# Gating the spatial and convolution branches, and splitting the products, in the projection phase instead of in the output tiles

## The chip, the core and the metric

The kernel runs on one core of a Trainium2 chip. The metric is the time on the device in microseconds, from launch to end. TensorE does the matmuls, VectorE (DVE), ScalarE (ACT) and GpSimd (POOL) the elementwise work, and SyncE (SP) issues all DMAs but two gathers.

## The reference

A decoder step with two layers. Each layer modulates its input of 2048 prompt tokens and 64 sample tokens (1024 features), projects it to 13 slabs, and runs four branches of 256 features: A, differential attention; B, a spatial-gating MLP; C, a convolution with 31 taps, LayerNorm, swish and a pointwise matmul; D, a gated recurrence (HGRN2). Every branch has a gate of its own, and the four products go through one output projection:

```python
o_a = o_a * silu(ag)
o_b = gelu(bu) * mixed(gelu(bv)) * silu(bg)
o_c = conv(cin) * silu(cg)
o_d = rms_norm(hgrn(dq, df, di)) * silu(dg)
mixed = concatenate([o_a, o_b, o_c, o_d]) @ w_out
y = layer_norm(ALPHA * x + gate * mixed)
```

The matmuls keep the accuracy of fp32 by splitting each operand into a high part (a cast to fp32r) and a low part (what the cast left out), and adding three products: high by high, low by high, high by low.

## The kernel before

**Phases.** Each layer has a projection phase in two groups of 1024 tokens (g=0, which also takes the 64 sample tokens, and g=1), and after it a phase of attention and output tiles. In the trace layer 0 projects until about 1010 us, attends until about 1620 us, layer 1 projects until about 2580 us and attends to the end.

**What the projection phase leaves in DRAM.** Gates are computed with features on the partitions: a matmul into PSUM, a tanh on ACT, `gate2` on DVE (L195), a store. `gate_slab` (L862) does so for the gate of D, `gate_pair` (L874) for those of A and C, and both store into the DRAM tensor `gat`. `gate_b` (L888) forms gelu(u) times the gate of B on POOL (L901) and stores that to `gat` too. A group has its tokens in blocks of 512 (with the sample tokens as well: 512, 288 and 288). The spatial mix of B (`b_v`, L906) and the convolution (`c_taps`, L1014, 30 multiply-adds on DVE per block at L1026; then `c_norm`, L1032) store their outputs in the DRAM tensor `catT`, features on rows. `c_norm` ends with a pointwise matmul (L1065), an ACT copy from PSUM (L1067, recorded at the helper's line L110) and a store.

**Output tiles.** `out_tile` (L1326) runs 17 times per layer, for 16 tiles of 128 prompt tokens and one of the 64 sample tokens. It multiplies branches by gates, splits the product in two parts and does the output matmuls (L1373 to L1375: high, low weight, low part). Half 0 (A and D) loads rows of `cat`, transposes them on TensorE and multiplies from PSUM on DVE (L1355). Half 1 (B and C) loads 512 rows of `gat` and of `catT` and multiplies on POOL:

```python
load(f4(gt), S.gat[g][half * 512:(half + 1) * 512, c0:c0 + M]...)   # L1337
load(f4(ct), S.catT[g][:, c0:c0 + M]...)                             # L1341
pick('EOT').tensor_tensor(tmp[:, cs], ct[:, cs], gt[:, cs], ALU.mult)  # L1349, POOL
cpy('EOH', hi[:, cs], tmp[:, cs])                                    # L1356, ACT cast, recorded at L110
sub_lo(..., lo[:, cs], tmp[:, cs], hi[:, cs])                        # L1357, POOL, recorded at L172
```

Loads and products live in staging tiles of 512 columns, "os" (4 buffers) and "zs" (5 buffers). "os" is shared with the loads of x in `build_h` (L453), which prepares the input of the next group.

**What sets the order.** Tile's scheduler orders the instructions of each engine from the program, its dependences, the buffers and the priorities in a table (L92 to L97), so an edit in one place can move rows elsewhere. All loads and stores stand in the one queue of SP. K, Q, V, the raw rows of `w_out` (cast on ACT at L1306, low part on POOL) and the vectors of the output LayerNorm (L1390, L1391 on POOL) are loaded into pools that open when the projection's pools close.

Of the kernel before, what the change touches and what calls it, by code (L numbers as in the profile page):

```python
# [9 lines left out]
F32 = mybir.dt.float32  # L10
F32R = mybir.dt.float32r
# [13 lines left out]
P = 128  # L25
# [43 lines left out]
def hymba_step_kernel(  # L69
# [60 lines left out]
    pool = L()  # L130
    pool.T2, pool.t2 = None, False
    uid = [0]

# [112 lines left out]
    def layer_scratch(l):  # L246
        s = L()
        s.qs = [[dram.tile([256, TG], F32, name=f"q{h}{l}_{g}") for h in "hl"] for g in range(NG)]
        s.ks = [[dram.tile([256, TG], F32, name=f"k{h}{l}_{g}") for h in "hl"] for g in range(NG)]
        s.vs = [dram.tile([512, 256], F32, name=f"v{l}_{b}") for b in range(T // 512)]  # L250
        s.catT = [dram.tile([512, RW], F32, name=f"catT{l}_{g}") for g in range(NG)]
        s.cat = [dram.tile([512, 512], F32, name=f"cat{l}_{b}") for b in range(T // 512)]
        s.gat = [dram.tile([D, RW], F32, name=f"gat{l}_{g}") for g in range(NG)]
# [607 lines left out]

    def gate_slab(l, g, h, col, row):  # L862
        w = slab(l, [(col, 256)])
        for m in range(2):
            for c0, n in blocks(g):
# [4 lines left out]
                gate2(o[:, 0:n], o[:, 0:n], ps[:, 0:n])  # L870
                store(scr[l].gat[g][row + m * P:row + (m + 1) * P, c0:c0 + n], o[:, 0:n])
                yield
# [15 lines left out]
    def gate_b(l, g, h, half):  # L888
        c = half * P
        w = slab(l, [(O_BU + c, P), (O_BG + c, P)])  # L890
        for c0, n in blocks(g):
# [9 lines left out]
            nc.gpsimd.tensor_tensor(a, a, b, ALU.mult)  # L901
            store(scr[l].gat[g][512 + c:512 + c + P, c0:c0 + n], a)
            yield
# [128 lines left out]
    def c_norm_(l, g, C, acc, t0, n, smpl, Lx):  # L1032
# [29 lines left out]
            for m in range(2):  # L1062
# [3 lines left out]
                o = C.pool.tile([P, 512], F32, tag="cn", name=nm("cn"), bufs=4)  # L1066
                cpy('ECO', o[:, 0:n], ps[:, 0:n])  # L1067
                r = TG if smpl else t0
                store(scr[l].catT[g][256 + m * P:256 + (m + 1) * P, r:r + n], o[:, 0:n])

# [255 lines left out]
    def out_tile(l, ti, O, last=False, act=None):  # L1326
# [7 lines left out]
        for half in (1, 0) if last else (0, 1):  # L1334
            f4 = lambda x: x[:, 0:4 * M].rearrange("p (k t) -> p k t", k=4)
            gt = st("os")
            load(f4(gt), S.gat[g][half * 512:(half + 1) * 512, c0:c0 + M].rearrange("(k p) t -> p k t", p=P))  # L1337
            ct, tmp = st("os"), st("os")
            hi, lo = st("zs", F32R), st("zs", F32R)
            if half:  # L1340
                load(f4(ct), S.catT[g][:, c0:c0 + M].rearrange("(k p) t -> p k t", p=P))  # L1341
            elif last:
# [3 lines left out]
            for k0, k1 in ((2, 4), (0, 2)) if last and not half else ((0, 4),):  # L1346
                cs = slice(k0 * M, k1 * M)
                if half:
                    pick('EOT').tensor_tensor(tmp[:, cs], ct[:, cs], gt[:, cs], ALU.mult)  # L1349
                else:  # L1350
                    ps = zt()
                    src = act if last and k0 == 0 else ct
                    for k in range(k0, k1):
                        nc.tensor.transpose(ps[:, k * M:(k + 1) * M], src[0:M, k * P:(k + 1) * P], ident[0:M, 0:M])
                    nc.vector.tensor_tensor(tmp[:, cs], ps[:, cs], gt[:, cs], ALU.mult)  # L1355
                cpy('EOH', hi[:, cs], tmp[:, cs])  # L1356
                sub_lo(nc.vector if last and not half else pick('EOL'), lo[:, cs], tmp[:, cs], hi[:, cs])  # L1357
                parts += [(O_K[half * 4 + k], f4(hi)[:, k, :], f4(lo)[:, k, :]) for k in range(k0, k1)]
        x = []
# [49 lines left out]
    for l in range(DEPTH):  # L1409
        with ExitStack() as ctx2:  # L1410
# [3 lines left out]
            for g in range(NG):  # L1414
# [38 lines left out]
                with tc.tile_pool(name=nm("cn"), reuse_waits="tile", bufs=1) as C.pool:  # L1453
                    todo = [(b * 512, 512, False) for b in range(NB)] + ([(0, NS, True)] if g == 0 else [])
                    accs = [c_taps(C, *todo[0], Lx)]
                    if g == 0:
                        with tc.tile_pool(name=nm("sap"), reuse_waits="tile", bufs=1) as sap:
                            prio(PSA, attention_sample, l, Lx, Sx, sap)
                    prio(KN['PGB'], run, gate_b(l, g, h, 0), gate_b(l, g, h, 1))
                    def mods():  # L1460
# [36 lines left out]
                    if KN['MO'] == 2:  # L1497
                        mods()
                if not KN['CS']:
                    c_state(l, g, C)  # L1500
# [74 lines left out]
```

## Time and profile before

| | |
|---|---|
| median of 3 runs | 3169.99 us (3167.98 to 3174.93) |
| the profiled execution | 3160.83 us |
| its span | 3159.1 us |
| granted TensorE clock, mean | 0.951 of full speed |
| busy: PE, DVE, ACT, POOL | 2828.0, 2235.2, 1162.9, 960.8 us |
| DMA: bytes moved, mean rate | 441.31 MB, 140 GB/s |

The profile covers one execution, from its first to its last instruction. Busy times are sums over the span, so they average stages with different limits. "Line" is the line of the program; helpers (L110 copies and casts on ACT, L172 subtractions that form low parts, L166 loads, L169 stores) collect operations of many places, and the tile names tell them apart.

### The profile page before, as it was taken

Reading aid. Unit: us, or ns where it says so; the run is one execution under the profiler, and the core shown is the slowest. Engines: PE = TensorE matmul, PEld = TensorE weight load, DVE = VectorE, ACT = ScalarE, POOL = GpSimd, SP = SyncE. Lnnn points to the kernel's source line nnn. Section 1 sums busy time; section 2 is a strip of 40 time slices with the busy share of each in tenths; the row PEclk is TensorE's granted clock in tenths of the full one; section 3 lists DMA queues with packets and bytes.
Section 4 is the critical chain, followed back from the end, with each engine's and each line's share of the span. In section 5 each row is a group of like instructions: output and inputs, shape, how many; then the busy total and the mean of one; then the engine's idle time right before and its main releaser. Section 6 shows DMA issues by size and latency. Waiting matters only on the chain. (4 is left out here: it accounts for less than half of the span.)

```text
span 3159.1 us, 55749 instructions
## 1 busy us (share of the span) xinstructions
PE 2828.0 (90%) x20888; PEld 2254.7 (71%) x20888; DVE 2235.2 (71%) x5280; ACT 1162.9 (37%) x2452; POOL 960.8 (30%) x1061
## 2 busy tenths in 40 slices
PE   5999989898999798888979999999999988997986
PEld 3888876788876566656668888767888856665665
DVE  2567883367583788879956678833676749898897
ACT  3212223211112666666641112232110146567663
POOL 3344364312011233404253344552120031332232
PEclk8999999899999899989989999999999988998998
DMA  6433544323555754446453335444334355444652
GB/s 237 147 128 108 173 146 154 108 92 128 174 180 203 184 133 112 118 112 166 122 197 111 122 119 192 140 139 124 117 120 140 117 166 123 129 118 108 158 155 67
DMA packets 323263, 441.31 MB, mean 140 GB/s; under 512 B 58704, under 2 KB 207734, under 8 KB 315811
## 3 DMA queue, kind: packets, MB, share of 16 engines
q1 hardware_dynamic: 316850, 420.97, 44.0%
q0 software_dynamic: 6144, 16.79, 1.8%
q8 instruction: 165, 2.70, 0.4%
q14 instruction: 104, 0.84, 0.1%
HBM read 295.80 MB, written 142.05 MB: 139 GB/s over the span
## 5 line engine op out<-in xcount | busy, mean ns | idle before, releaser
L525 PE MATMUL z<-hh,wh 128*128 128x512 f32 (+1 forms) x1440 | 528.4, 367 | 17.1 <-DVE zs L195 9.1
L527 PE MATMUL z<-hh,wl 128*128 128x512 f32 (+1 forms) x1440 | 522.1, 363 | 0.0
L526 PE MATMUL z<-hl,wh 128*128 128x512 f32 (+1 forms) x1440 | 518.6, 360 | 0.0
L516 PE MATMUL z<-wh,hh 128*128 128x256 f32 (+1 forms) x1360 | 399.9, 294 | 16.0 <-ACT wh L110 4.3
L686 ACT ACTIVATE P<-S,stt 128x1024 f32<-128x1024 f32 (+7 forms) x384 | 332.7, 868 | 182.1 <-DVE stt L682 120.0
L518 PE MATMUL z<-wh,hl 128*128 128x256 f32 (+1 forms) x1360 | 394.7, 290 | 0.0
L517 PE MATMUL z<-wl,hh 128*128 128x256 f32 (+1 forms) x1360 | 393.9, 290 | 0.6 <-POOL wl L172 0.6
L682 DVE TENSOR_REDUCE stt<-S 128x1 f32<-128x1024 f32 (+7 forms) x384 | 344.0, 904 | 64.2 <-PE S L680 48.7
L1026 DVE SCALAR_TENSOR_TENSOR acc<-glu,cw,acc 128x512 f32<-128x512 f32 x480 | 378.0, 834 | 3.3
L525 PEld LDWEIGHTS z<-hh,wh 128*128 128x128 f32 x1440 | 275.7, 191 | 80.1 <-issue 14.4
L527 PEld LDWEIGHTS z<-hh,wl 128*128 128x128 f32 x1440 | 275.5, 191 | 44.7 <-issue 7.0
L526 PEld LDWEIGHTS z<-hl,wh 128*128 128x128 f32 x1440 | 275.7, 191 | 42.7 <-issue 6.3
L678 PE MATMUL S<-K,Q 128*128 128x512 f32 (+3 forms) x640 | 229.2, 430 | 77.1 <-ACT P L686 61.6
L516 PEld LDWEIGHTS z<-wh,hh 128*128 128x128 f32 (+1 forms) x1360 | 262.3, 193 | 25.9 <-issue 5.7
L517 PEld LDWEIGHTS z<-wl,hh 128*128 128x128 f32 (+1 forms) x1360 | 261.9, 193 | 4.9 <-issue 2.6
L518 PEld LDWEIGHTS z<-wh,hl 128*128 128x128 f32 (+1 forms) x1360 | 261.5, 192 | 2.3 <-issue 0.3
L172 POOL TENSOR_TENSOR wl<-raw,wh 128x512 fp32r<-128x512 f32 x112 | 150.8, 1362 | 256.5 <-ACT wh L110 218.2
L1373 PE MATMUL z<-woh,zs 128*128 128x512 f32 (+1 forms) x480 | 202.7, 422 | 24.0 <-ACT zs L110 15.1
L1375 PE MATMUL z<-woh,zs 128*128 128x512 f32 (+1 forms) x480 | 200.2, 417 | 10.0 <-POOL zs L172 9.8
L730 PE MATMUL X<-ph,V 128*64 128x128 f32 x2176 | 196.1, 294 | 10.4 <-ACT ph L727 9.8
L678 PEld LDWEIGHTS S<-K,Q 128*128 128x128 f32 x640 | 114.9, 204 | 122.1 <-ACT P L686 90.0
L725 PE MATMUL T<-cst,P 128*128 128x128 f32 x1088 | 189.2, 302 | 13.3 <-DVE P L707 8.8
(374 smaller groups left out, 5410.5 us busy)
## 6 DMA issues: line engine op xcount, KB each, us to landing
wp<-wh SPq DMA_DIRECT2D x28, 1024.0 KB
wp<-wl SPq DMA_DIRECT2D x28, 1024.0 KB
wh<-wp SPq DMA_DIRECT2D x56, 512.0 KB
wl<-wp SPq DMA_DIRECT2D x56, 512.0 KB
K<-kh SPq DMA_DIRECT2D x224, 128.0 KB
K<-kl SPq DMA_DIRECT2D x224, 128.0 KB
mw<-in_w_ada_dram SPq DMA_DIRECT2D x24, 1024.0 KB
raw<-in_w_in_dram SPq DMA_DIRECT2D x64, 256.0 KB
```

The source lines that it names most:

```text
L516: nc.tensor.matmul(ps, hh[:, k, tok:tok + M], wh[:, k, :], start=(k == 0), stop=False)
L517: nc.tensor.matmul(ps, hh[:, k, tok:tok + M], wl[:, k, :], start=False, stop=False)
L518: nc.tensor.matmul(ps, hl[:, k, tok:tok + M], wh[:, k, :], start=False, stop=(k == KT - 1))
L525: nc.tensor.matmul(ps, wh[:, k, ms], hh[:, k, c0:c0 + n], start=(k == 0), stop=False)
L526: nc.tensor.matmul(ps, wh[:, k, ms], hl[:, k, c0:c0 + n], start=False, stop=False)
L527: nc.tensor.matmul(ps, wl[:, k, ms], hh[:, k, c0:c0 + n], start=False, stop=(k == KT - 1))
L678: nc.tensor.matmul(s[:, o:o + w], qt[:, m, :], kst[pc * 2 + o // 512][:, m, 0:w], start=True, stop=not diag)
L682: nc.vector.tensor_reduce(col(m, pc), s[:, :n], AX.X, ALU.max, negate=True)
L686: nc.scalar.activation(p[:, :n], s[:, :n], AF.Exp, bias=col(m, pc), scale=1.0, accum_out=l1 if m == 0 and npc == 1 else col(m, 2 + pc))
L1026: nc.vector.scalar_tensor_tensor(av, src(j), Lx.cw[:, c, j:j + 1], av, op0=ALU.mult, op1=ALU.add)
L1373: nc.tensor.matmul(po[0:M], a, wh[:, k, :], start=(i == 0), stop=False)
L1375: nc.tensor.matmul(po[0:M], b, wh[:, k, :], start=False, stop=(i == KT - 1))
```

## The change

In each layer the product of branch and gate, and its split in two parts, is made once per block of the projection phase for B and C, and the parts go to new DRAM tensors `bc` (high and low). `gat` keeps the gates of A and D, `catT` the spatial mix, and `gc` holds the gate of C. `gate_b` loads the mix and multiplies on DVE; `c_norm` loads the gate of C and multiplies from PSUM on DVE, where ACT copied. Each then casts on ACT, subtracts on POOL and stores both parts. The gate of C is now computed ahead of those of A and D. In g=0 the parts are staged in "os"; in g=1 in a pool of their own, "tp", with 6 buffers. Half 1 of an output tile only loads two parts.

```diff
+    def tp_row(dt=F32):
+        return pool.tp.tile([P, 512], dt, tag="tp", name=nm("tp"), bufs=NTP) if pool.tp else st("os", dt)
+
+    def two_parts(l, g, r, c0, n, x):
+        hi, lo = tp_row(F32R)[:, 0:n], tp_row(F32R)[:, 0:n]
+        nc.scalar.copy(hi, x)
+        sub_lo(nc.gpsimd, lo, x, hi)
+        for part, dst in zip((hi, lo), scr[l].bc[g]):
+            store(dst[r:r + P, c0:c0 + n], part)
...
             nc.gpsimd.tensor_tensor(a, a, b, ALU.mult)
-            store(scr[l].gat[g][512 + c:512 + c + P, c0:c0 + n], a)
+            ct = tp_row()[:, 0:n]
+            load(ct, scr[l].catT[g][c:c + P, c0:c0 + n])
+            nc.vector.tensor_tensor(a, a, ct, ALU.mult)
+            two_parts(l, g, c, c0, n, a)
             yield
...
-                cpy('ECO', o[:, 0:n], ps[:, 0:n])
                 r = TG if smpl else t0
-                store(scr[l].catT[g][256 + m * P:256 + (m + 1) * P, r:r + n], o[:, 0:n])
+                load(o[:, 0:n], scr[l].gc[g][m * P:(m + 1) * P, r:r + n])
+                nc.vector.tensor_tensor(o[:, 0:n], ps[:, 0:n], o[:, 0:n], ALU.mult)
+                two_parts(l, g, 256 + m * P, r, n, o[:, 0:n])
...
         for half in (1, 0) if last else (0, 1):
...
             hi, lo = st("zs", F32R), st("zs", F32R)
             if half:
-                load(f4(ct), S.catT[g][:, c0:c0 + M].rearrange("(k p) t -> p k t", p=P))
+                for part, src in zip((hi, lo), S.bc[g]):
+                    load(f4(part), src[:, c0:c0 + M].rearrange("(k p) t -> p k t", p=P))
+                parts += [(O_K[4 + k], f4(hi)[:, k, :], f4(lo)[:, k, :]) for k in range(4)]
+                continue
...
+                    if g == NG - 1:
+                        ctx3 = ExitStack()
+                        pool.tp = ctx3.enter_context(tc.tile_pool(name=nm("tp"), reuse_waits="tile", bufs=1))
...
-                    gp = chain(gate_slab(l, g, h, *((O_DG, 256), (O_AG, 0), (O_CG, 768))[KN['GO']]), gate_pair(l, g, h, *(((O_AG, 0), (O_CG, 768)), ((O_DG, 256), (O_CG, 768)), ((O_AG, 0), (O_DG, 256)))[KN['GO']]))
+                    gp = chain(gate_c(l, g, h), gate_pair(l, g, h, (O_AG, 0), (O_DG, 256)))
```

`gate_c` is `gate_slab` cut to the gate of C, with its store to `gc`. The changed program's lines are numbered 1 to 21 higher.

**POOL, output tiles of layer 0.** Before, a tile has three rows: the low part of half 0 (`zs_13509`), the product of half 1 at L1349, and its low part (`zs_13524`); `x` rows are the LayerNorm of the tile before.

```order
406 L1390 TENSOR_TENSOR x_12031<-x_12031,lng_10813 128x512
407 L1391 TENSOR_TENSOR x_12031<-x_12031,lnb_10814 128x512
408 L172 TENSOR_TENSOR zs_13509<-os_13507,zs_13508 128x512
409 L1349 TENSOR_TENSOR os_13522<-os_13521,os_13519 128x512
410 L172 TENSOR_TENSOR zs_13524<-os_13522,zs_13523 128x512
411 L1390 TENSOR_TENSOR x_12116<-x_12116,lng_10813 128x512
```

```order
414 L1409 TENSOR_TENSOR x_12132<-x_12132,lng_10969 128x512
415 L1409 TENSOR_TENSOR x_12163<-x_12163,lng_10969 128x512
416 L1410 TENSOR_TENSOR x_12132<-x_12132,lnb_10970 128x512
417 L1410 TENSOR_TENSOR x_12163<-x_12163,lnb_10970 128x512
418 L173 TENSOR_TENSOR zs_13631<-os_13634,zs_13630 128x512
```

The same tile has one row now, the low part of half 0.

**SP, end of g=0 in layer 0.** `os` from `in_x_prompt_dram` are the loads of x for g=1; before, four of them come behind the convolution's store of the block.

```order
243 L169 DMA catT_0_142<-cn_6042 128x512
244 L169 DMA gat_0_148<-zs_6104 128x288
245 L166 DMA os_6162<-in_x_prompt_dram 128x512
246 L166 DMA os_6176<-in_x_prompt_dram 128x512
247 L169 DMA catT_0_142<-cn_6047 128x512
248 L166 DMA os_6189<-in_x_prompt_dram 128x512
```

```order
254 L167 DMA cn_6125<-gc_0_144 128x512
255 L170 DMA gat_0_150<-zs_6188 128x288
256 L170 DMA bch_0_152<-os_6117 128x512
257 L170 DMA bcl_0_153<-os_6118 128x512
258 L170 DMA bch_0_152<-os_6128 128x512
259 L167 DMA os_6192<-in_x_prompt_dram 128x512
260 L167 DMA os_6206<-in_x_prompt_dram 128x512
261 L170 DMA bcl_0_153<-os_6129 128x512
262 L167 DMA os_6219<-in_x_prompt_dram 128x512
```

Now the four "os" buffers hold the two parts of both rows of that block, and eight loads of x come behind their stores.

**SP, end of the projection in layer 1.** Before, half of the raw `w_out` rows are loaded between gate stores, ahead of the convolution's last stores.

```order
1103 L169 DMA gat_1_191<-zs_25989 128x512
1104 L166 DMA raw_26895<-in_w_out_dram 128x512
1105 L166 DMA raw_26899<-in_w_out_dram 128x512
1112 L166 DMA raw_26923<-in_w_out_dram 128x512
1113 L169 DMA catT_1_185<-cn_26059 128x512
```

```order
1201 L170 DMA bcl_1_203<-tp_26322 128x512
1202 L170 DMA bch_1_202<-tp_26332 128x512
1203 L170 DMA bcl_1_203<-tp_26333 128x512
1204 L167 DMA V_26499<-v_0_186 128x4x256
1205 L167 DMA raw_27077<-in_w_out_dram 128x512
1206 L167 DMA raw_27081<-in_w_out_dram 128x512
```

Now V and all sixteen raw rows come behind the last stores out of "tp".

## Rows read from the trace of the kernel before

**Rows 1.** The page: the span, and each engine's busy time.

```profile
span 3159.1 us, 55749 instructions
PE 2828.0 (90%) x20888; PEld 2254.7 (71%) x20888; DVE 2235.2 (71%) x5280; ACT 1162.9 (37%) x2452; POOL 960.8 (30%) x1061
```

**Rows 2.** Windows, both attention phases: stretch, length, busy per engine, clock, DMA share, GB/s.

```profile
1010.00:1620.00 610.00, 520.59 (x3142) 375.42 (x3142) 503.10 (x1269) 373.04 (x801) 192.29 (x151) 0.93 0.54 143
2580.00:3159.00 579.00, 495.25 (x3065) 358.08 (x3063) 501.16 (x1253) 357.23 (x769) 156.44 (x122) 0.93 0.48 125
```

**Rows 3.** Groups of instructions on POOL, and those of the out tiles on PE.

```profile
L172 POOL TENSOR_TENSOR zs<-os,zs 128x512 fp32r<-128x512 f32 (+1 forms) x64 | 83.8, 1315 | 230.8 <-ACT zs L110 222.6 <-PE S L1374 6.8 <-issue 1.3
L1349 POOL TENSOR_TENSOR os<-os,os 128x512 f32<-128x512 f32 (+1 forms) x34 | 43.2, 1272 | 147.8 <-DMA os<-catT 64.2 <-DVE stt L684 22.8 <-PE S L678 18.3
L1373 PE MATMUL z<-woh,zs 128*128 128x512 f32 (+1 forms) x480 | 202.7, 422 | 24.0 <-ACT zs L110 15.1 <-DVE t L1377 8.3
L1375 PE MATMUL z<-woh,zs 128*128 128x512 f32 (+1 forms) x480 | 200.2, 417 | 10.0 <-POOL zs L172 9.8
L110 ACT CAST zs<-os 128x512 fp32r<-128x512 f32 (+1 forms) x72 | 42.2, 586 | 49.8 <-POOL os L1349 26.9 <-DVE os L1355 16.7 <-PE S L1375 6.3
```

**Rows 4.** Timeline of POOL, 1037 to 1043 us: start, us, engine, line, what.

```profile
1037.97 4.05 POOL L172 TENSOR_TENSOR wol<-raw,woh 128x512 fp32r<-128x512 f32 x3 [9.55 <-PE S L678]
```

**Rows 5.** Timeline of DVE, 1037 to 1061 us.

```profile
1038.72 0.54 DVE L698 SCALAR_TENSOR_TENSOR stt<-ls,nlam,stt 128x1 f32<-128x1 f32 x1
1039.30 1.59 DVE L712 SCALAR_TENSOR_TENSOR P<-P,stt,P 128x384 f32<-128x384 f32 x1
...
1041.19 0.84 DVE L698 SCALAR_TENSOR_TENSOR stt<-ls,nlam,stt 128x1 f32<-128x1 f32 x1
...
1054.74 0.62 DVE L712 SCALAR_TENSOR_TENSOR P<-P,stt,P 128x384 f32<-128x384 f32 x1
...
1060.40 0.22 DVE L698 SCALAR_TENSOR_TENSOR stt<-ls,nlam,stt 128x1 f32<-128x1 f32 x1
```

**Rows 6.** One line's durations, minimum, median and maximum in ns: the taps.

```profile
L1026 DVE SCALAR_TENSOR_TENSOR acc<-glu,cw,acc x480: 719/743/3359, 345.8 to 2502.0; 128x512 f32<-128x512 f32 x160
```

**Rows 7.** The tile `raw` from 2300 us on: the rows of `w_out` in layer 1.

```profile
L172 POOL TENSOR_TENSOR wol<-raw,woh x16: 1253/1287/1782, 2528.7 to 2572.9; 128x512 fp32r<-128x512 f32 x16
```

**Rows 8.** The chain that ended last, 2744 to 2757 us: start, us, what.

```profile
2747.16 1.62 SPq L166
...
2749.29 3.16 DMA os<-catT
...
2752.62 1.26 POOL os L1349
...
2754.60 1.29 POOL zs L172
```

**Rows 9.** Groups on DVE and POOL by form, for the sizes of the added work.

```profile
L195 DVE SCALAR_TENSOR_TENSOR zs<-zs,z 128x512 f32<-128x512 f32 x48 | 32.7, 682 | 76.0 <-ACT zs L883 68.7 <-ACT zs L869 6.4 <-ACT zs L899 0.6
L195 DVE SCALAR_TENSOR_TENSOR zs<-zs,z 128x288 f32<-128x288 f32 x32 | 14.3, 448 | 26.6 <-ACT zs L883 14.9 <-ACT zs L869 6.5 <-ACT zs L899 4.9
```

**Rows 10.** Windows in the projections (g=0 and g=1 of both layers), and layer 1's end.

```profile
400.00:450.00 50.00, 45.12 (x278) 38.09 (x277) 50.00 (x76) 12.28 (x23) 24.75 (x13) 0.97 0.41 143
850.00:900.00 50.00, 50.00 (x224) 38.98 (x223) 47.04 (x71) 3.59 (x6) 1.74 (x1) 1.00 0.34 113
1950.00:2000.00 50.00, 47.41 (x272) 39.33 (x271) 50.00 (x76) 13.60 (x25) 21.01 (x15) 1.00 0.41 139
2450.00:2500.00 50.00, 50.00 (x217) 40.23 (x216) 49.20 (x70) 5.39 (x9) 6.38 (x4) 1.00 0.35 116
2550.00:2580.00 30.00, 20.39 (x68) 10.85 (x68) 12.59 (x24) 11.50 (x21) 12.97 (x11) 0.77 0.66 173
```

**Rows 11.** Timeline of PE, 588 to 600 us, where the input of g=1 is built.

```profile
588.59 1.11 PE L460 MATMUL S<-cst,os 128*128 128x128 f32 x4 [2.44 <-DMA os<-in_x_prompt_dram]
591.30 1.94 PE L460 MATMUL S<-cst,os 128*128 128x128 f32 x8 [1.59 <-DMA os<-in_x_prompt_dram]
```

More of the change, by code (lines that the diff above doesn't have):

```diff
@@ L131, in hymba_step_kernel @@
     pool.T2, pool.t2 = None, False
+    pool.tp, NTP = None, 6
     uid = [0]
@@ L250, in layer_scratch @@
         s.vs = [dram.tile([512, 256], F32, name=f"v{l}_{b}") for b in range(T // 512)]
-        s.catT = [dram.tile([512, RW], F32, name=f"catT{l}_{g}") for g in range(NG)]
+        s.catT = [dram.tile([256, RW], F32, name=f"catT{l}_{g}") for g in range(NG)]
+        s.gc = [dram.tile([256, RW], F32, name=f"gc{l}_{g}") for g in range(NG)]
         s.cat = [dram.tile([512, 512], F32, name=f"cat{l}_{b}") for b in range(T // 512)]
-        s.gat = [dram.tile([D, RW], F32, name=f"gat{l}_{g}") for g in range(NG)]
+        s.gat = [dram.tile([512, RW], F32, name=f"gat{l}_{g}") for g in range(NG)]
+        s.bc = [[dram.tile([512, RW], F32, name=f"bc{h}{l}_{g}") for h in "hl"] for g in range(NG)]
         s.y = [dram.tile([P, D], F32, name=f"y{l}_{b}") for b in range(NT)]
@@ L859, in attention_sample, with gate_c @@
         store(scr[l].cat_s[:, 0:256], on[0:NS, 0:256])
-    def gate_slab(l, g, h, col, row):
-        w = slab(l, [(col, 256)])
+    def tp_row(dt=F32):
[6 more added lines that the diff above has]
+            store(dst[r:r + P, c0:c0 + n], part)
+    def gate_c(l, g, h):
+        w = slab(l, [(O_CG, 256)])
         for m in range(2):
@@ L870, in gate_slab @@
                 gate2(o[:, 0:n], o[:, 0:n], ps[:, 0:n])
-                store(scr[l].gat[g][row + m * P:row + (m + 1) * P, c0:c0 + n], o[:, 0:n])
+                store(scr[l].gc[g][m * P:(m + 1) * P, c0:c0 + n], o[:, 0:n])
                 yield
@@ L1335, in out_tile @@
             f4 = lambda x: x[:, 0:4 * M].rearrange("p (k t) -> p k t", k=4)
-            gt = st("os")
-            load(f4(gt), S.gat[g][half * 512:(half + 1) * 512, c0:c0 + M].rearrange("(k p) t -> p k t", p=P))
-            ct, tmp = st("os"), st("os")
             hi, lo = st("zs", F32R), st("zs", F32R)
             if half:
-                load(f4(ct), S.catT[g][:, c0:c0 + M].rearrange("(k p) t -> p k t", p=P))
-            elif last:
+                for part, src in zip((hi, lo), S.bc[g]):
+                    load(f4(part), src[:, c0:c0 + M].rearrange("(k p) t -> p k t", p=P))
+                parts += [(O_K[4 + k], f4(hi)[:, k, :], f4(lo)[:, k, :]) for k in range(4)]
+                continue
+            gt, ct, tmp = st("os"), st("os"), st("os")
+            load(f4(gt), S.gat[g][:, c0:c0 + M].rearrange("(k p) t -> p k t", p=P))
+            if last:
                 load(ct[:, 256:512], tok_rows(S.cat, ti, 1)[:, 256:512])
@@ L1345, in out_tile @@
                 load(ct[0:M], S.cat_s if smpl else tok_rows(S.cat, ti, 1))
-            for k0, k1 in ((2, 4), (0, 2)) if last and not half else ((0, 4),):
+            for k0, k1 in ((2, 4), (0, 2)) if last else ((0, 4),):
                 cs = slice(k0 * M, k1 * M)
[L1348 to L1355, printed above, removed]
+                ps = zt()
+                src = act if last and k0 == 0 else ct
+                for k in range(k0, k1):
+                    nc.tensor.transpose(ps[:, k * M:(k + 1) * M], src[0:M, k * P:(k + 1) * P], ident[0:M, 0:M])
+                nc.vector.tensor_tensor(tmp[:, cs], ps[:, cs], gt[:, cs], ALU.mult)
                 cpy('EOH', hi[:, cs], tmp[:, cs])
-                sub_lo(nc.vector if last and not half else pick('EOL'), lo[:, cs], tmp[:, cs], hi[:, cs])
-                parts += [(O_K[half * 4 + k], f4(hi)[:, k, :], f4(lo)[:, k, :]) for k in range(k0, k1)]
+                sub_lo(nc.vector if last else pick('EOL'), lo[:, cs], tmp[:, cs], hi[:, cs])
+                parts += [(O_K[k], f4(hi)[:, k, :], f4(lo)[:, k, :]) for k in range(k0, k1)]
         x = []
@@ L1498, in hymba_step_kernel @@
                         mods()
+                    if g == NG - 1:
+                        pool.tp = None
+                        ctx3.close()
                 if not KN['CS']:
```

## The prediction

> **What bounds the kernel now.** I read the page first, then the windows, then the groups of instructions, the chain of waits, and single stretches in the timeline. The page shows PE busy 2828 of 3159 us and DVE 2235 [rows 1]; PE looks like the bound and the edit removes no matmul. The windows show where it is not. In the two attention phases, 1189 us together, PE stands idle for 89 and 84 us, DVE is busy 82% and 87%, ACT about 61%, POOL 32% and 27% [rows 2]. There PE and DVE bound each other in turn, a score tile at a time. In the projections PE fills the window at g=1 (50.00 of 50), while at g=0 DVE is full and PE lacks 4.9 and 2.6 us per 50 [rows 10].
>
> The groups tell what the edited operations do to PE directly: the high-part matmuls of the output tiles wait 15.1 us for ACT casts, the low-part ones 9.8 us for POOL's subtraction [rows 3], both halves counted. The chain of waits shows one such place: `catT` lands after 3.16 us, POOL multiplies for 1.26, subtracts for 1.29, and PE starts after it [rows 8].
>
> The indirect effect is larger. Between 1037.97 and 1042.02 POOL works for 4.05 us [rows 4]. In it DVE's L712 on 384 columns takes 1.59 us, and L698, a single column, 0.54 and 0.84. Later in the same phase, away from POOL's work, the same forms take 0.62 and 0.22 [rows 5]. DVE loses 0.97 + 0.32 + 0.62 = 1.91 us to 4.05 us of POOL: **0.47 us of DVE per us of POOL**. That rate is the centre of my sum; it is one sample, and its ends are 0 and 1.
>
> **The change part by part.** Sums are against the profiled execution, 3160.83 us (span 3159.1); it lies 9 us below the median of the runs, 3169.99, and I put the same difference on both.
>
> *1. Output tiles, DVE freed of POOL.* Removed are 34 products (43.2 us in all) and 34 subtractions (34 x 1.315 = 44.7) [rows 3], together 87.9 us of POOL, half per layer, and 34 casts of 0.586 us on ACT, 20 us, where ACT has room. At 0.47 DVE gets back 41 us, 20.7 per layer. PE and DVE being busy to about the same share, I count half of DVE's relief: -10.3 us per layer. In layer 1 something goes against it. The sixteen low parts of `w_out` are made from 2528.7 to 2572.9 us, ahead of attention [rows 7]; the order puts their loads behind the last stores out of "tp", so they fall into the first attention heads, as they already do in layer 0. Sixteen at 1.287 us are 20.6 us of POOL, 9.7 of DVE, half of it +4.8. Together -10.3 - 10.3 + 4.8 = **-15.8**. Ends: 0, if PE is the bound all the same, and -41 + 10 = -31, if DVE is.
>
> *2. Output tiles, the direct waits.* Of 15.1 + 9.8 = 24.9 us [rows 3] about half belong to half 1, 12.5. The parts now come by two loads into "zs", which has five buffers while a tile takes four; the loads wait for the matmuls of the tile before, and then land as late as `catT` did, 3.16 us [rows 8]. The loads are the same bytes as those they replace, and what goes is the 2.55 us behind them. I take **-5**; ends 0 and -12.5.
>
> *3. Added work in the projections.* Per layer `gate_b` gets six products of 512 columns and four of 288. Nearest rows are the two-operand L195, 682 and 448 ns [rows 9]: 5.9 us of DVE. `c_norm` gets eight of 512 and two of 64 columns, about 5.9 us. Twenty subtractions (14 at about 1.3 us, four of 288 at some 0.75, two small) are some 21.7 us of POOL and take 10.2 us of DVE at 0.47. So DVE gets 22 us more per layer, 44 in all. The ten ACT casts more per layer (`c_norm`'s copy goes, every block gets a cast) lie in slots where ACT is busy about a quarter of the time or less [rows 10]. At g=1 PE has no gap for it to widen. At g=0 DVE is full, and `gate_b`'s share there is about half of (5.9 + 5.1) x 2 = 22, so 11 us; I count a third: **+4**. Ends 0 and +22, all of `gate_b`'s share. The extra loads and stores (88 more rows in SP's order) add about 17 MB (four times 256 rows of 2112 tokens per layer); the DMA engines are busy half of the time [rows 2], and I cost the bytes at nothing. If that cover were gone, 17 MB at 143 GB/s would be 120 us of traffic, which would show first as waits for K and weights.
>
> *4. From g=0 to g=1.* PE already waits here 2.44 and 1.59 us for x to land [rows 11]. In "os" the eight last loads of x now come behind the stores of the convolution's parts. From the pointwise matmul on, product, cast and subtraction (0.68 + 0.59 + 1.32 = 2.6 us) stand ahead of the store, where one copy of about 0.6 stood, and store and load then land in turn at about 3.16 each [rows 8]. So the loads could be 2 + 3.2 + 3.2 = 8.4 us later, if nothing of it is hidden; the first eight loads and the gate matmuls beside them hide most. I take +3 per layer, **+6**; ends 0 and +17.
>
> *5. From g=1 to attention.* V, `w_out` and the LayerNorm vectors wait until "tp" is free. The K loads do not. So the first scores start on time, and the sample's output tile, which in layer 1 filled slots of PE's end (20.39 of 30 us busy, [rows 10]), moves behind the first head. I take **+2**; ends 0 and +10, the idle time of that window.
>
> Sum: -15.8 - 5 + 4 + 6 + 2 = -8.8, rounded to -9: 3152 for the profiled execution, and 3169.99 - 9 = **3161 us** for the median.
>
> **A rule against the change.** The row shows DVE slowed by POOL, not stopped: 1.59 us for work of 0.62 beside subtractions of 1.35 each [rows 4, 5], and a tap goes from 743 ns to as much as 3359 [rows 6]. The Trainium skill, page "SBUF — State Buffer", section "Who interferes with whom", says of such a pair that the lock is exclusive: a DVE instruction with two operands in SBUF and a GpSimd instruction that reads SBUF exclude each other for a whole instruction, whoever starts first; a DVE instruction with one operand in PSUM is left alone. By that rule each us of POOL could cost up to one of DVE rather than 0.47, so that part 1 would be an estimated -33 in place of -15.8, and the new subtractions beside the taps would cost DVE 22 us per layer rather than 10; the attention's part of it is what rival B comes to from the rows. The trace agrees with it in kind, even for one column; the amount I take from the rows.
>
> **The rivals.**
>
> *A, the forecast,* -9, own range -20 to 0: 3150 to 3170. Chance 0.42.
>
> *B, DVE is the whole bound in attention.* Its relief then counts in full, -31, and the direct waits fully, -12.5, against +12 of parts 3 to 5: -32, 3138 us. For it: DVE at 87% in layer 1 [rows 2]. Against: PE's 85%. Chance 0.17.
>
> *C, a load takes the place of the chain.* Two parts into five "zs" buffers arrive late behind K and Q in SP's queue, where the chain shows an issue that lasts 1.62 us [rows 8]; the direct waits stay, and a quarter of DVE's relief counts, -8: -8 + 12 = +4, 3174 us, give or take 6. For it: POOL waited 64.2 us for `catT` before [rows 3], so these loads were late already, but with POOL's time to spare. Chance 0.18.
>
> *D, slower: DVE sets the end of the projections.* If taps, gates and the new work on DVE end later than PE's matmuls, the 44 us of part 3 count instead of 4. With the attention's gain as forecast that is -9 + 40 = +31; if only `gate_b`'s 22 count, +9. Middle: +20, 3190 us. It decides where PE waits on DVE in the convolution's tail. For it: DVE at 49 and 47 of 50 at the ends of both projections [rows 10]. Against: PE is at 50.00 there too. Chance 0.23.
>
> That the change does not do what it says I give no chance: the order has no product of half 1 on POOL any more, and 28 rows fewer there.
>
> **How the numbers follow.** A measurement of this kernel tells about 0.2%, 6.3 us, from no change. Of A, 0.30 lies more than that below 3170 and 0.12 within. B is faster, 0.17. Of C 0.12 is within and 0.06 slower. D is slower, 0.23. So faster 0.47, same 0.24, slower 0.29. The range, 3134 to 3192, takes in A, C, most of B and most of D, and leaves out some 0.07 below and 0.09 above; A's own range stands with it.
>
> **What would show it.** In the profile after: POOL in both attention phases some 40 us lower in layer 0 and 20 in layer 1; DVE there about 20 and 10 us less busy; the wait of low-part matmuls for POOL at about half of 9.8; PE's windows there fuller. For part 3, DVE's sum in the projections up by about 44 us, PE unchanged at g=1. For part 4, waits of L460's matmuls for x above 2.44 us. I am wrong if DVE's busy time in attention falls and PE's idle time does not (C), if the phases before 1010 and from 1620 to 2580 us grow by 10 us or more each (D), or if new waits for `bch` and `bcl` appear ahead of the output matmuls.

## The result and the profile after

The changed kernel takes 3194.9 us (median of 5 runs, 3190.19 to 3199.46) where the kernel before takes 3169.99: a ratio of **1.0074, interval 1.0056 to 1.0093**. It is slower, the forecast was 9 us faster, and the time lies 3 us above the range. The profiled execution took 3190.76 us, 30 more than that of before.

The page of the changed kernel, against [rows 1]: POOL is 54 us and DVE 11 us less busy, and the span is 30 us longer.

```profile
span 3189.0 us, 55868 instructions
PE 2841.3 (89%) x20888; PEld 2262.1 (71%) x20888; DVE 2224.7 (70%) x5320; ACT 1157.5 (36%) x2438; POOL 906.8 (28%) x1033
```

Where the time went is read from PE's timeline in both traces, as the way between matmuls that every version has. "Gates of g=0" runs from the start of the last projection matmul with 256 columns in g=0 to that of the first in g=1; "g=1" from there to the last gate matmul; "attention" of layer 0 from there to the last matmul with 256 columns in layer 1's g=0, that of layer 1 to the end. The first column is in us, the others are differences to it:

| stretch | before | changed | e1 | e3 | e8 |
|---|---|---|---|---|---|
| layer 0, gates of g=0 | 268.6 | +15.0 | +0.5 | +2.2 | +15.4 |
| layer 0, g=1 | 420.2 | -1.3 | -0.2 | +3.6 | -1.6 |
| layer 0, attention | 881.0 | -13.3 | -11.9 | -12.4 | -9.5 |
| layer 1, gates of g=0 | 265.7 | +18.8 | +10.6 | +8.4 | +20.0 |
| layer 1, g=1 | 388.2 | +0.2 | -0.1 | +4.2 | +4.2 |
| layer 1, attention and end | 605.0 | +7.9 | -8.7 | +1.8 | -2.6 |

(e1, e3 and e8 are experiments below, on chips where the kernel before took about the same. The first 330 us differ by 0 to 4. Each column is one execution: in e4, whose output tiles are those of the changed kernel, layer 0's attention came out at -3.7, so a few us in one stretch are within the scatter.) Two stretches lost 34 us, layer 0's attention won 13, and layer 1's, which was to win as well, lost 8.

The windows over both attention phases of the changed kernel, against [rows 2], and the start of layer 1's:

```profile
1026.00:1624.00 598.00, 519.58 (x3150) 374.64 (x3149) 477.79 (x1270) 368.32 (x789) 150.73 (x120) 0.92 0.56 149
2600.00:3189.00 589.00, 504.23 (x3087) 365.83 (x3086) 484.27 (x1254) 359.32 (x770) 133.18 (x107) 0.91 0.51 134
2600.00:2650.00 50.00, 39.69 (x187) 24.49 (x187) 36.85 (x98) 32.95 (x92) 22.75 (x18) 0.71 0.87 235
```

In layer 0 POOL (192 to 151 us) and DVE (503 to 478) fell as forecast, and PE's idle time went from 89 to 78 us. In layer 1 POOL fell by 23 only, and the first 50 us have PE at 39.7 and a granted clock of 0.71. At about the same distance from its last gate matmul the kernel before had 41.8 and 0.83:

```profile
2580.00:2630.00 50.00, 41.82 (x227) 28.09 (x225) 39.65 (x138) 31.14 (x96) 6.60 (x6) 0.83 0.54 148
```

Two groups of output matmuls and POOL's subtraction of the changed kernel, against [rows 3]:

```profile
L1392 PE MATMUL z<-woh,zs 128*128 128x512 f32 (+1 forms) x480 | 200.8, 418 | 21.3 <-DMA zs<-bch 14.1 <-DVE t L1396 5.1 <-ACT woh L1326 0.9
L1394 PE MATMUL z<-woh,zs 128*128 128x512 f32 (+1 forms) x480 | 196.6, 410 | 3.8 <-POOL zs L173 3.6
L173 POOL TENSOR_TENSOR zs<-os,zs 128x512 fp32r<-128x512 f32 (+1 forms) x30 | 37.2, 1239 | 328.7 <-ACT zs L110 257.2 <-DMA K<-kl 22.8 <-issue 22.0
```

The wait for the cast (15.1 us) became a wait for the load of `bch` (14.1); the wait for POOL fell from 9.8 to 3.6.

The end of g=0 in layer 0, from the timelines of DVE, SP and PE of the changed kernel. The last row of PE is the first projection matmul of g=1:

```profile
583.06 0.69 DVE L1088 TENSOR_TENSOR cn<-S,cn 128x512 f32<-128x512 f32 x1 [2.28 <-DMA cn<-gc]
586.81 0.69 DVE L815 TENSOR_REDUCE sms<-X 128x1 f32<-128x512 f32 x1 [3.05 <-PE T L809]
...
590.14 0.68 DVE L1088 TENSOR_TENSOR cn<-S,cn 128x512 f32<-128x512 f32 x1
```

```profile
584.43 0.32 SPq L170 DMA_DIRECT2D bch<-os  x1
585.83 0.32 SPq L170 DMA_DIRECT2D bcl<-os  x1
591.50 0.32 SPq L170 DMA_DIRECT2D bch<-os  x1
591.91 0.88 SPq L167 DMA_DIRECT2D os<-in_x_prompt_dram  x2
592.88 0.38 SPq L170 DMA_DIRECT2D bcl<-os  x1
593.50 11.54 SPq L167 DMA_DIRECT2D os<-in_x_prompt_dram  x6
```

```profile
597.79 1.07 PE L851 MATMUL T<-osel,cst 128*32 128x256 f32 x4 [0.56 <-DVE osel L848]
598.79 1.97 PE L464 MATMUL S<-cst,os 128*128 128x128 f32 x8
...
608.65 2.16 PE L464 MATMUL S<-cst,os 128*128 128x128 f32 x8 [2.46 <-ACT zs L480]
...
616.35 0.56 PE L520 MATMUL z<-wh,hh 128*128 128x256 f32 x1
```

The kernel before has the first and the last of these rows earlier:

```profile
583.77 0.63 PE L847 MATMUL T<-osel,cst 128*32 128x256 f32 x4
...
598.79 0.56 PE L516 MATMUL z<-wh,hh 128*128 128x256 f32 x1
```

The second row of the convolution is multiplied 7 us after the first, because DVE's order has the sample attention (L812 to L823) between them; its parts are stored at 591.5 and later, and the last eight loads of x, which need the same four "os" buffers, all come after that. The 8.4 us that I had as an end for a layer and the 7 us between the two products would make about the 15.0 measured. That sum is an argument and not shown, and it does not come out in layer 1, where 4.6 us lie between the products and 18.8 were lost. A second thing came with the change: the end of the sample attention (the matmuls of the tile `osel`) started 6 us after the last gate matmul of g=0 before and starts 19 us after it now, and PE makes the last transposes of x (L464) behind it. e11 has the parts in "os" without the late sample attention, e12 the late sample attention without the parts in "os".

### The profile page after: what moved, and what is told of

It reads as the page before. It is cut to its first block, busy times and chain, and to the rows that moved or that the text cites. A ratio compares the mean times of both kernels' runs of the same rounds, so it can differ in the third digit from the quotient of the medians.

```text
span 3189.0 us, 55868 instructions
## 1 busy us (share of the span) xinstructions
PE 2841.3 (89%) x20888; PEld 2262.1 (71%) x20888; DVE 2224.7 (70%) x5320; ACT 1157.5 (36%) x2438; POOL 906.8 (28%) x1033
## 5 line engine op out<-in xcount | busy, mean ns | idle before, releaser
L520 PE MATMUL z<-wh,hh 128*128 128x256 f32 (+1 forms) x1360 | 397.4, 292 | 12.7 <-ACT wh L110 4.0
L1045 DVE SCALAR_TENSOR_TENSOR acc<-glu,cw,acc 128x512 f32<-128x512 f32 x480 | 387.5, 850 | 3.1
L529 PEld LDWEIGHTS z<-hh,wh 128*128 128x128 f32 x1440 | 275.5, 191 | 74.5 <-DVE zs L196 16.6
L1392 PE MATMUL z<-woh,zs 128*128 128x512 f32 (+1 forms) x480 | 200.8, 418 | 21.3 <-DMA zs<-bch 14.1
L731 ACT COPY ph<-T 128x512 f32<-128x512 f32 (+2 forms) x320 | 161.0, 522 | 124.9 <-PE T L729 122.8
```

The lines of the kernel that those rows point to most:

```text
L520: nc.tensor.matmul(ps, hh[:, k, tok:tok + M], wh[:, k, :], start=(k == 0), stop=False)
L529: nc.tensor.matmul(ps, wh[:, k, ms], hh[:, k, c0:c0 + n], start=(k == 0), stop=False)
L1045: nc.vector.scalar_tensor_tensor(av, src(j), Lx.cw[:, c, j:j + 1], av, op0=ALU.mult, op1=ALU.add)
L1392: nc.tensor.matmul(po[0:M], a, wh[:, k, :], start=(i == 0), stop=False)
```

## Experiments

The kernel before took 3168 and 3172 us on the chips of the first eight runs, and 3192 and 3194 on those of the last seven; so times are compared by the ratio to before on the same chip. Brackets are 95% intervals. In the profiles of the last seven the first 330 us, ahead of the gates, are already 8 to 12 us longer than in the profile before, so their stretches, given as differences to that profile, hold a share of the chip's. Five runs compute something else: in e1, e6, e9 and e13 B and C enter the output matmuls without their product, and in e2 the two parts are multiplied with each other. Lines of the diffs are shortened, with subscripts left out.

**One half of the change each.** e1 has the output tiles of the change on the projection of before, e2 the opposite.

```diff
             if half:
-                load(f4(ct), S.catT[g][:, c0:c0 + M]...)
+                for part, src in zip((hi, lo), (S.gat[g][512:1024], S.catT[g])):
+                    load(f4(part), src[:, c0:c0 + M]...)
+                parts += ...; continue
```

> The kernel before, with one part of the change alone: half 1 of an output tile loads the rows of gat and of catT straight into the two zs tiles, with no product, cast or subtraction (so B and C enter the output matmuls unmultiplied). Theory 1 (the output tiles gain what was forecast, DVE freed of POOL, and the projection loses more): 16 to 40 us faster than before, 3130 to 3154, with POOL some 44 us lower and DVE some 20 us lower in each attention phase. Theory 2 (the output tiles gain nothing, a load takes the place of the chain): 3164 to 3176.

Measured: 0.9959 (0.9937 to 0.9981). The windows over both attention phases of e1:

```profile
1020.00:1613.00 593.00, 516.00 (x3138) 372.77 (x3138) 475.58 (x1267) 367.22 (x793) 153.38 (x119) 0.92 0.55 146
2580.00:3153.00 573.00, 498.81 (x3066) 362.73 (x3064) 465.17 (x1252) 350.89 (x755) 110.37 (x90) 0.92 0.48 126
```

Against [rows 2] POOL is 39 and 46 us lower, DVE 28 and 36, and by the table attention is 12 and 9 us shorter: theory 1. Only 13 us show in the total, since layer 1's gates of g=0, which e1 does not touch, took 10.6 us longer (below).

```diff
+                gt, ct, tmp = st("os"), st("os"), st("os")
+                for part, src in zip((gt, ct), S.bc[g]): load(f4(part), ...)
+                pick('EOT').tensor_tensor(tmp, ct, gt, ALU.mult)
+                cpy('EOH', hi, tmp); sub_lo(pick('EOL'), lo, tmp, hi)
```

> The changed kernel, with the other part alone: the projection phase makes and stores the parts, and half 1 of an output tile still loads two operands into os and multiplies, casts and subtracts them as before (so the output matmuls get the product of the two parts). Theory 1: the loss of the projection phases and of the transitions shows undiminished, 45 to 65 us over before, 3215 to 3235, with e1 and e2 adding up to the change's +25. Theory 2: 3190 to 3200, as the changed kernel.

Measured: 1.018 (1.0149 to 1.021), 58 us more. The loss lies in the projection and what follows it; -13 and +58 add up to +45, not to +25: layer 1's attention is 25.1 us longer than before here, where it is 7.9 longer in the change and 8.7 shorter in e1. Why the parts don't add up there isn't shown.

**Staging.** The four pieces of the diff are those of e3, e4, e8 and of e6 and e7. e3 puts the convolution's parts of g=0 into "cn" tiles; e4 gives the gate's load its own tile; e8 drops the pool "tp"; e5 is e3 and e8; e6 and e7 load the low part into "os", on e1 and e5.

```diff
-                two_parts(l, g, 256 + m * P, r, n, o[:, 0:n])
+                    hi = C.pool.tile([P, 512], F32R, tag="cn", name=nm("cn"), bufs=5)[:, 0:n]
+                    lo = C.pool.tile([P, 512], F32R, tag="cn", name=nm("cn"), bufs=5)[:, 0:n]
...
-                load(o[:, 0:n], scr[l].gc[g][m * P:(m + 1) * P, r:r + n])
+                gl = C.pool.tile([P, 512], F32, tag="gl", name=nm("gl"), bufs=1)
+                load(gl[:, 0:n], scr[l].gc[g][m * P:(m + 1) * P, r:r + n])
...
-                        pool.tp = ctx3.enter_context(tc.tile_pool(name=nm("tp"), reuse_waits="tile", bufs=1))
...
-            hi, lo = st("zs", F32R), st("zs", F32R)
+            hi, lo = st("zs", F32R), st("os" if half else "zs", F32R)
```

> The changed kernel, but in g=0 the parts of the convolution are staged in cn tiles (5 buffers instead of 4) and not in os, so that the loads of x for g=1 don't share buffers with them. If the os buffers hold up the x loads (theory 1): the way from the last gate matmul of g=0 to the first projection matmul of g=1 shortens by 5 to 10 us in each layer, 3175 to 3187. If DVE's added work sets the end of the projection (rival D): no change, 3190 to 3199.

Measured: 1.0026 (1.0005 to 1.0046), some 15 us of the 25 gone. The first matmul of g=1 in e3:

```profile
601.36 0.56 PE L520 MATMUL z<-wh,hh 128*128 128x256 f32 x1
```

The gates of g=0 are 12.8 and 10.4 us shorter than in the changed kernel, more than the 5 to 10 expected. DVE's work is the same in both, so rival D is not what cost this. (e3's g=1 took 3.6 and 4.2 us longer than before, by the table, and holds back part of the gain.)

> The changed kernel, but the gate of C is loaded into a tile of its own and not into the cn tile that takes the product, so the load need not wait until a cn buffer is free. If the late load of the gate holds up the end of both groups (theory 1, second part): the products in c_norm no longer wait for the load (2.28 us in g=0 of layer 0, 4.80 us of PE at the end of layer 1's projection), 4 to 12 us faster than the changed kernel, 3183 to 3191. If it is the staging in os alone: 3190 to 3199.

Measured: 1.0076 (1.0047 to 1.0106), no gain, and the gates of g=0 still take 14.4 and 17.7 us more than before. The gate's load is not what holds the stretch up.

> The changed kernel without the pool tp: in g=1 the parts are staged in os too, where no loads of x compete, so that the memory of V, w_out and the output vectors is not held by tp. In layer 1 the first raw rows of w_out come 97 rows earlier in SP's queue than in the changed kernel. If the late w_out and sample tile cost the start of attention in layer 1 (28 us between the first and the 96th score matmul against before): 10 to 25 us faster than the changed kernel, 3170 to 3185. If attention is slowed there for another reason: 3190 to 3199.

Measured: 1.0048 (1.0025 to 1.007), a gain of some 8 us over the changed kernel, less than the 10 to 25 expected, and with intervals that overlap. In layer 1's attention 10.5 of the 16.6 us by which the changed kernel lies above e1 come back. The low parts of `w_out` in layer 1, first of the changed kernel, then of e8, against [rows 7]:

```profile
L173 POOL TENSOR_TENSOR wol<-raw,woh x16: 1262/1273/1737, 2610.6 to 2644.9; 128x512 fp32r<-128x512 f32 x16
```

```profile
L173 POOL TENSOR_TENSOR wol<-raw,woh x16: 1259/1275/1809, 2557.7 to 2602.5; 128x512 fp32r<-128x512 f32 x16
```

The last gate matmul starts at 2554.0 before, at 2576.0 in the changed kernel and at 2583.2 in e8. So e8 has the low parts where they lay before, from 25 us ahead of it to 19 behind, and the changed kernel has them 35 to 69 us behind. Still, from the first to the 96th score matmul of layer 1 e8 takes 141.2 us, where the changed kernel takes 148.5, before 122.2 and e1 120.8. The late `w_out` is thus not what holds most of that start up; what does stays open.

> Both edits of e3 and e8: the convolution's parts of g=0 in cn tiles, everything of g=1 in os, no tp. If the two are separate losses, they add up: e3's 23 us and e8's gain below the changed kernel, 3145 to 3162, faster than before. If e3 already holds what there is to gain: 3166 to 3175.

Measured: 1.0022 (1.0005 to 1.0039): as e3, the two gains do not add up. The gates of layer 0 keep e3's gain (+3.4), but layer 1's g=1 is 9.9 us longer than before. What does that is open.

> e1 (only the output tiles changed) with the low part of half 1 loaded into os instead of zs, so that a tile takes three of the five zs buffers and not four. If the load waits for a zs buffer of the tile before it (rival C, seen at the end of layer 1, where e1 takes 64.4 us from the last score matmul to the end and the kernel before 55.8): the end shortens by 5 to 9 us, 3140 to 3150. If it is something else: 3152 to 3160, as e1.

Measured: 0.9988 (0.9968 to 1.0008), no gain over e1, whose interval overlaps; the expected 5 to 9 us do not show. From the last score matmul to the end it takes 65.5 us, no less than e1. The "zs" buffers are not what holds the end up.

> e5 with the low part of half 1 in os, as in e6: all three repairs together. If the three losses are separate: 5 to 10 us below e5, 3138 to 3155, and faster than before by 0.4 to 0.9%. If one bound holds them all: as e5.

Measured: 1.0009 (0.9991 to 1.0028), as before. None of these repairs of the staging makes the change a gain.

**Why the output tiles gain.** e9 is e1 with POOL's work put back on results that nobody reads.

```diff
+                idle = st("os")
+                nc.gpsimd.tensor_tensor(idle, hi, lo, ALU.mult)
+                nc.gpsimd.tensor_tensor(idle, hi, lo, ALU.subtract)
```

> e1 (the output tiles alone changed), but POOL still multiplies and subtracts two 512-column operands for every half 1, on the loaded parts, into an os tile that nobody reads. If e1's gain is DVE freed of POOL: the gain goes, 3162 to 3172, and DVE's busy time in the attention phases is back at 500 us or more. If the gain is the shorter way from load to matmul (casts and subtractions that PE waits for): e1's time stays, 3150 to 3160.

Measured: 1.0069 (1.0056 to 1.0082). The gain is gone, and more. The pages' busy times of e1 and of e9, which have the same 5280 instructions on DVE as the kernel before [rows 1]:

```profile
PE 2829.2 (90%) x20888; PEld 2262.2 (72%) x20888; DVE 2169.2 (69%) x5280; ACT 1146.6 (36%) x2418; POOL 879.4 (28%) x993
```

```profile
PE 2848.5 (89%) x20888; PEld 2270.3 (71%) x20888; DVE 2228.1 (69%) x5280; ACT 1146.2 (36%) x2418; POOL 968.2 (30%) x1061
```

DVE gets back 66 us from before to e1, and loses 59 again when 89 us of POOL return in e9: 0.66 us per us of POOL, where I had read 0.47. This speaks for DVE's relief as the gain of the output tiles, and against the shorter way to the matmul, which e9 keeps. It does not prove it: e9 is even slower than before, which isn't explained and lies outside what DVE's relief had let me expect, so something besides DVE's time was put back too. Its POOL stands 118.3 us before these products, waiting for the loads, with its later work behind them:

```profile
L1342 POOL TENSOR_TENSOR os<-zs,zs 128x512 f32<-128x512 f32 (+1 forms) x34 | 45.6, 1341 | 118.3 <-DMA zs<-catT 118.3
```

**Which part of the added work loses.** e10 gates and splits the spatial branch alone, e11 the convolution alone; e12 makes both products in the projection and stores them whole, with the split left in the output tiles. None has "tp". First e10's piece of `c_norm`, then e11's of `gate_b`, then e12's:

```diff
-                load(o[:, 0:n], scr[l].gc[g][m * P:(m + 1) * P, r:r + n])
-                nc.vector.tensor_tensor(o[:, 0:n], ps[:, 0:n], o[:, 0:n], ALU.mult)
-                two_parts(l, g, 256 + m * P, r, n, o[:, 0:n])
+                cpy('ECO', o[:, 0:n], ps[:, 0:n])
+                store(scr[l].cc[g][m * P:(m + 1) * P, r:r + n], o[:, 0:n])
...
-            nc.vector.tensor_tensor(a, a, ct, ALU.mult)
-            two_parts(l, g, c, c0, n, a)
+            store(scr[l].cc[g][c:c + P, c0:c0 + n], a)
...
-                two_parts(l, g, 256 + m * P, r, n, o[:, 0:n])
+                store(scr[l].bc[g][256 + m * P:256 + (m + 1) * P, r:r + n], o[:, 0:n])   # e12, and so in gate_b
...
+                ct = st("os")
+                load(f4(ct), S.bc[g][:, c0:c0 + M]...)
+                cpy('EOH', hi, ct); sub_lo(pick('EOL'), lo, ct, hi)
```

> Only the spatial branch is gated and split in the projection phase (gate_b), staged in os, with no pool tp; the convolution stays as before, and an output tile still multiplies, casts and subtracts its 256 columns. If the loss sits in the convolution's parts, which stand between the last gates and the loads of x: no loss from g0 to g1 (within 3 us of before in layer 0), about half of e1's gain, 3158 to 3167. If the gate's order or gate_b's parts share in the loss: 3170 to 3185.

Measured: 0.9999 (0.9983 to 1.0015). Layer 0's gates of g=0 take 1.7 us more than before, as expected; half of e1's gain does not appear.

> The counterpart: only the convolution's output is gated and split in the projection phase, staged in os, no tp; the spatial branch is multiplied in the output tiles as before. If the loss sits in the convolution's parts: 10 us or more longer from the gates of g=0 to the first projection matmul of g=1 in each layer, 3175 to 3190. If it takes both halves to fill os: 3160 to 3172.

Measured: 1.0053 (1.0033 to 1.0073). Layer 0's gates take 19.9 us more than before. Of these 13.1 lie behind the last gate matmul, where PE now waits for the loads of x longer than the 2.44 and 1.59 us of [rows 11]:

```profile
599.24 0.63 PE L852 MATMUL T<-osel,cst 128*32 128x256 f32 x4 [0.56 <-DVE osel L849]
608.73 1.11 PE L465 MATMUL S<-cst,os 128*128 128x128 f32 x4 [8.87 <-DMA os<-in_x_prompt_dram]
611.98 1.97 PE L465 MATMUL S<-cst,os 128*128 128x128 f32 x8 [2.14 <-DMA os<-in_x_prompt_dram]
```

The sample attention ends early here, as before, so this is the price of the convolution's parts in the "os" buffers. The other 6.8 us lie ahead of the last gate matmul, beside a POOL product of 17.0 us of the kind shown below.

> The products are made in the projection phase as in the change, but stored whole: the split (ACT cast, POOL subtraction) stays in the output tiles, which load one operand instead of two and lose POOL's product. No parts are staged in os, c_norm gets a load and DVE's product in place of ACT's copy, and there is no tp. If the split's staging is the loss and the products cost nothing: the way from g=0 to g=1 as before within 4 us in layer 0, half of e1's gain in attention, 0.2 to 0.5% faster than before. If the gate's load and the product behind the pointwise matmul are the loss: 0.2 to 0.6% slower than before.

Measured: **0.9918 (0.9904 to 0.9932)**, 25 us faster than before and 1.5% below the changed kernel: better than either. The first stretch is back (-0.2 us), the attention phases are 6.5 and 10.6 us shorter than in the profile before, and on this chip the kernel before is 24 us slower than there. Against e15, which has the attention phases of the kernel before and ran on the same chip, they are 12.7 and 14.1 us shorter. Its windows and POOL's subtractions:

```profile
1025.00:1629.00 604.00, 520.52 (x3181) 377.82 (x3180) 496.32 (x1276) 376.34 (x812) 173.44 (x136) 0.92 0.53 142
2575.00:3158.00 583.00, 502.86 (x3100) 364.82 (x3098) 484.51 (x1260) 361.89 (x777) 145.18 (x111) 0.93 0.47 122
```

```profile
L173 POOL TENSOR_TENSOR zs<-os,zs 128x512 fp32r<-128x512 f32 (+1 forms) x64 | 83.4, 1312 | 350.0 <-ACT zs L110 269.8 <-PE T L729 43.6 <-PE S L1395 13.6
```

POOL keeps its 64 subtractions and loses only the 34 products, and a tile loads one operand of half 1 instead of two; which of the two gives the gain was not separated. The products made early cost nothing at the end of layer 0's g=0; the split staged in "os" does, and staged in "cn" tiles (e3) it costs 2.2 us there.

Layer 1's gates of g=0 are still 10.2 us longer than in the profile before in e12, 11.9 in e10 and 8.4 in e3. From PE's timelines, in us after the end of the last gate matmul of g=0, layer 0 and layer 1:

| | before | changed | e3 | e11 | e12 |
|---|---|---|---|---|---|
| last matmul of `osel` starts | 6.3, 7.9 | 19.0, 19.6 | 20.2, 21.6 | 6.5, 8.3 | 20.3, 22.4 |
| first projection matmul of g=1 | 21.1, 20.0 | 37.1, 39.1 | 26.2, 29.0 | 34.2, 32.8 | 23.6, 30.0 |

So what e3 and e12 still lose comes with the sample attention behind the last gates, 2.5 to 5.1 us in layer 0 and 9 to 10 in layer 1. No run moves the sample attention alone; that it is the cause is not shown.

**POOL starved by the taps.** In e1's layer 1 the gates of g=0 lost 10.6 us. POOL's timeline in e1, PE's after it, and POOL's same product in layer 1 of the kernel before:

```profile
1998.47 17.02 POOL L901 TENSOR_TENSOR zs<-zs,zs 128x512 f32<-128x512 f32 x1 [8.64 <-DVE zs L195]
...
2026.57 0.99 POOL L787 DMA_INDIRECT Ks<-in_cache_k_dram,pidx  x1 [0.16 <-issue]
```

```profile
2029.47 0.45 PE L793 MATMUL T<-cst,Ks 128*128 128x128 f32 x1 [11.75 <-DMA Ks<-in_cache_k_dram,pidx]
```

```profile
2005.06 8.69 POOL L901 TENSOR_TENSOR zs<-zs,zs 128x512 f32<-128x512 f32 x1 [8.64 <-DVE zs L195]
```

e13 to e15 make that product on DVE, in e1, e12 and the kernel before.

```diff
-            nc.gpsimd.tensor_tensor(a, a, b, ALU.mult)
+            nc.vector.tensor_tensor(a, a, b, ALU.mult)
```

> e1 (output tiles alone) with gate_b's product of gelu(u) and gate on DVE instead of POOL. In e1 one such product on POOL took 17.0 us beside DVE's run of taps (8.7 before), the gathers of cached keys stood behind it, and PE waited 11.75 us. If that is what e1 lost in layer 1's g=0 (10.6 us against before): the loss goes, 0.7 to 0.9% faster than before. If the wait moves elsewhere: as e1, 0.3 to 0.5% faster.

> e12 with gate_b's product on DVE as well, so that POOL has no two-operand instruction beside the taps there but the weight splits. If the starved product matters in e12 too: 0.2 to 0.4% below e12; if e12 does not starve POOL: within 0.2% of it.

> The kernel before with gate_b's product on DVE and nothing else, the control for e13 and e14. Its longest product on POOL took 8.7 us, twice, without a wait of PE on it beyond 1.24 us: no change, within 0.2% of before. If those products held up POOL's gathers: 0.2 to 0.4% faster.

Measured: e13 0.9878 (0.9861 to 0.9895), e14 0.9928 (0.9914 to 0.9942), e15 0.9971 (0.9956 to 0.9987). In e13 layer 1's gates of g=0 lie 2.6 us above before instead of 10.6, and the gain is 1.2% instead of 0.4%, more than expected (e1 ran on another chip), and more than the one wait of 11.75 us accounts for; the rest is open. The kernel before gains 0.3% from the same edit, where I had expected nothing. e13 and e15 differ in the output tiles alone and lie 0.9% apart, some 29 us of 3194. In e12, where no such product took over 1.75 us, the edit brings nothing, as expected.

## Why the prediction was wrong

By its own steps:

- **Step 1, DVE freed of POOL, was right in mechanism and about right in size.** -10.3 us forecast for layer 0, with -2.5 for half of step 2; 13.3 measured. In layer 1 e1 shows 8.7. That the sizes agree so closely is luck: e4 shows 3.7 in layer 0 with the same tiles, and two errors cancel. DVE's relief itself was larger than my 41 us (66 from before to e1, 0.66 per us of POOL in e9), and less of it reached the end than the half I counted.
- **Step 2** came out near its size by another way. Waits of the two groups went from 34.0 to 25.1 us (-8.9 where I took -5), but the wait for a cast was replaced by one for the load (14.1 us), which is rival C's mechanism at a smaller price, and one of the signs that I had named.
- **Step 3 was right in sum, and rival D wrong.** The 120 taps of a stretch in layer 0 took 125 us at g=0 and 100 at g=1 before, 134 and 105 after, by their first and last starts, and g=1 got no longer (-1.3 and +0.2 us). DVE's busy time outside the windows of attention rose by 32 us, 44 forecast. The sign that I had set for D, both projection phases longer by 10 us or more, did show, but for the reason of step 4.
- **Step 4 is the step that failed first.** I took +3 per layer of up to 8.4 for the loads of x behind the parts' stores and wrote that the first eight loads and the gate matmuls hide most. The stretch lost 15.0 and 18.8. e3, with the parts in tiles of their own, takes back 12.8 and 10.4, and e11, with the convolution's parts alone, loses 13.1 behind the last gate matmul of layer 0: more than the 8.4, so nothing of it was hidden. The order of SP was in front of me, and I priced its chain without DVE's order between the two products. The 2.2 and 8.4 us that e3 still loses come with the sample attention moved behind the last gates, which no step priced; their cause is not shown.
- **Step 5 is the second.** I took +2 for what comes behind "tp", and counted the late `w_out` only as half of DVE's share of POOL's time (+4.8 in step 1). Layer 1's attention came out 16.6 us longer than in e1; dropping "tp" gives 10.5 back. The late `w_out` is not the larger part of it: e8 has it back in its place, and the first 96 score matmuls still take 19 us longer than before. Which row holds them up stays open.

So the slower result came with a gain in layer 0's attention near the forecast size, and from two places that the text had named and sized too low: +34 instead of +6, of which e3 takes back 23, and +17 instead of +7, of which e8 takes back 10.5. Rival D, which held most of the chance of slower, was not what happened. The rule against the change did not decide either. The stretches of taps grew by 9 and 5 us, but hardly by the new subtractions: in e12, which has none of these, they take 131 and 105 us. In layer 0 the taps themselves sum to 107.7 us at g=0 before and 105.8 after, and to 92.3 and 96.0 at g=1; at g=0 the growth is DVE's other work between them, 21.1 us before and 33.0 after. The gates of g=0 in layer 0 ended no later for it (246.4 us after the last projection matmul with 256 columns, 247.4 before).

## What to carry to other kernels

Where a step is moved into an earlier phase, follow each of its buffers to the next user: here the parts took the four staging tiles that the next group's loads needed, and the pool for them held back loads of the phase after. Ask what shrinks on the way: here the product alone (0.9918) did better than product and split (1.0074), since the product halves the bytes that the later tile loads, while the split doubles them again and adds a cast, a subtraction and a store at a place with no room. And when a change of code in one place shows a loss in another, look there for an instruction whose duration jumped.

## What the runs showed of the hardware

A POOL instruction beside a run of two-operand DVE instructions can be held for many of them: the same product took 1.73 us in the median, 8.69 once in each layer before, and 17.02 in e1, e6, e9 and e11, beside DVE's runs of taps. The Trainium skill, page "SBUF — State Buffer", section "Who interferes with whom", has such a pair exclude each other for a whole instruction; the trace agrees, and shows that the wait is not over after one: in layer 1, ten taps start within the 8.69 us and twenty-two within the 17.02. DVE's rows where these two waits end, first before, then e1:

```profile
2009.22 3.38 DVE L1026 SCALAR_TENSOR_TENSOR acc<-glu,cw,acc 128x512 f32<-128x512 f32 x5
2013.96 0.45 DVE L195 SCALAR_TENSOR_TENSOR zs<-zs,z 128x288 f32<-128x288 f32 x1 [1.35 <-ACT zs L899]
```

```profile
2006.30 8.02 DVE L1026 SCALAR_TENSOR_TENSOR acc<-glu,cw,acc 128x512 f32<-128x512 f32 x12
2015.96 0.46 DVE L195 SCALAR_TENSOR_TENSOR zs<-zs,z 128x288 f32<-128x288 f32 x1 [1.64 <-ACT zs L899]
```

The last taps end at 2012.60 and 2014.32, DVE pauses, and the products end at 2013.75 and 2015.49, 1.15 and 1.17 us into the pause; a product of this size in the output tiles took 1.27 in the mean [rows 3]. In layer 0 of the kernel before, the same wait ends without such a pause, and the next tap takes 1.40 us. The price falls on whatever stands behind in POOL's queue, here the gathers.
